# Two MLPs as Strassen quads: seven block products in place of eight, with the residual and the hidden layer in DRAM

## The chip, the cores and the metric

The kernel runs on one core of one Trainium2 chip. The metric is the device time of one execution in microseconds; a median over several executions stands for a kernel. The engines are TensorE (PE, with its weight load PEld), VectorE (DVE), ScalarE (ACT), GpSimd (POOL) and SyncE (SP), which here issues all transfers.

## The reference

Two layers over 1024 tokens of width 1024 in fp32. In each a mixer (another one in each layer), a cross attention on a memory, and an MLP add to the residual `x`; a last norm ends it. The change is in the MLPs (4096 hidden columns):

```python
def rmsnorm(x, g):
    xf = x.astype(jnp.float32)
    y = xf * lax.rsqrt(jnp.mean(xf * xf, axis=-1, keepdims=True) + EPS)
    return (y * g.astype(jnp.float32)).astype(x.dtype)

def sq_relu_mlp(h, w1, w2):
    return jnp.square(jax.nn.relu(h @ w1)) @ w2

    for l in range(DEPTH):
...
        x = x + mem_cross_attn(rmsnorm(x, xa_norm[l]), memn, xa_wq[l], xa_wk[l], xa_wv[l], xa_wo[l])
        x = x + sq_relu_mlp(rmsnorm(x, mlp_norm[l]), mlp_w1[l], mlp_w2[l])
    return rmsnorm(x, final_norm)
```

## The kernel before

Everything is feature-major: a tile is 128 features by 512 tokens, and the tokens come in two halves. The residual is 16 such tiles, which stay in SBUF from the first addition of a layer to its end. fp32 operands are split into two parts, `hi` (a cast to fp32r on ScalarE) and `lo` (the source minus `hi`, a subtraction), and each 128x128 by 128x512 product is three matmuls: hi·hi, hi·lo, lo·hi (`mm3`, L149 to L151).

Weights come as tiles of 128x1024 (512 KB) through `ldw`: the load, the cast on ScalarE (L142), the subtraction on GpSimd (L143). The program's six parts run one after the other: mix0, xa0 (cross attention), mlp0, mix1, xa1, mlp1 with the last norm.

`mlp` first splits the residual times the gain (`split_half`, L233 and L234; the factor 1/rms is left for later) and makes 1/rms of every token (`norm_stat`: squares L176, their sum L178, a matmul with ones L187, L192, a power on GpSimd L195, the diagonal L207, a matmul L208, and a copy L212 into `yy`). The part for half 0 of the tokens stands first; that for half 1 waits as `pending` while the work on half 0 goes on. Then come eight chunks of 512 hidden columns. In a chunk `up` makes 4 tiles for both halves (8 × 3 matmuls each), takes each out of PSUM with one VectorE operation (L1355: max with 0, times `yy`), squares it (L1359, ScalarE), and splits it (L1361 ScalarE, L1362 VectorE); `down` makes 8 output tiles for both halves (4 × 3 matmuls each) and adds them to the residual (L251). That is 192 + 192 = 384 matmuls a chunk, 3072 a layer. `lagged` orders the items so that the second half runs one or two items behind the first. Names in the rows: `hh`/`hl` are the parts of the normed input, `wr`/`wh`/`wl` a weight raw and its parts, `L` the parts of the hidden layer, `mm` a PSUM bank, `x` a residual tile.

The order of instructions on each engine is set by the framework's scheduler, which works with a modelled timeline and lets lines under `high_priority()` go first. On the chip each engine, and SP's list of transfers, runs its list in order.

Of the kernel before, what the change touches and what calls it, by code (L numbers as in the profile page):

```python
# [26 lines left out]
class Model:  # L27
    def __init__(self, ctx, tc, a):
        self.tc, self.nc, self.a = tc, tc.nc, a
        self.const = ctx.enter_context(tc.tile_pool(name="const", bufs=1))  # L30
# [150 lines left out]
    def rms(self, xs, n, ss, eng, scale=1.0):  # L181
        """scale / rms of every token, tokens on partitions: a column for each 128."""
# [15 lines left out]
    def norm_stat(self, xs, n, bank, eng, copy=True):  # L198
        """1/rms of every token, on all partitions (by a product with a diagonal) and as rms() has it."""
# [53 lines left out]
    def lagged(self, items, load, do, head=1, tail=1):  # L253
        """do(item, tile, half) for both halves, the second one an item behind (head and tail: at the ends)."""
# [13 lines left out]
    def proj(self, w, half, tag=None):  # L268
        """[128 columns, 512 tokens] in PSUM: w holds [128, 8, 128]."""
# [7 lines left out]
    # ---------------------------------------------------------------- pieces  # L277
# [60 lines left out]
    def mix_start(self, l, bank, right):  # L338
        """hT and 1/rms, and the residual's place to the tags in right."""
# [34 lines left out]
    def ab_consts(self):  # L374
# [8 lines left out]
        # neg_tri[s', s] = -1 for s' >= s  # L383
# [4 lines left out]
        # mask_diag[s, t] = -1e30 for s >= t  # L388
# [26 lines left out]
    def scaled(self, t, ps, half, scale=1.0):  # L415
        """t = scale * ps / rms."""
# [3 lines left out]
    def spill(self, i, w, half, scale=1.0, fn=None, tag=None):  # L420
        """One projected tile, through fn(t), to DRAM scratch."""
# [11 lines left out]
    def out_parts(self, gated):  # L433
        """The heads' outputs in parts, where hT was."""
# [32 lines left out]
    # ---------------------------------------------------------------- mLSTM  # L467
    def ml_gates(self):
# [30 lines left out]
        # tanh(x / 15) = 1 - 2 / (exp(2 x / 15) + 1)  # L499
# [21 lines left out]
        # running maximum of a within each chunk, chunks and heads on partitions  # L521
# [11 lines left out]
        # maxima carried from chunk to chunk, on one partition  # L533
# [22 lines left out]
        # w_old of head 2p on partitions 0-63 and of head 2p+1 on 64-127  # L556
# [30 lines left out]
    def ml_heads(self, p):  # L587
        nc = self.nc
        C = None
        for half in HALVES:  # L590
# [3 lines left out]
            for i in range(4):  # L594
# [3 lines left out]
                # queries of the two heads on a diagonal of blocks, keys, queries for the state  # L598
# [104 lines left out]
    # ---------------------------------------------------------------- stick breaking  # L703
# [29 lines left out]
    def sb_attn(self, h):  # L733
# [3 lines left out]
        for Q in HALVES:  # L737
# [9 lines left out]
            for j in range(4 * Q + 3, -1, -1):  # L747
# [10 lines left out]
                # softplus(z) = max(z, 0) + log(1 + exp(-|z|))  # L758
# [46 lines left out]
    # ---------------------------------------------------------------- gated delta rule  # L805
# [34 lines left out]
        # what a doubling from 32 to 64 and one from 64 to 128 multiplies, zero outside of the blocks  # L840
# [3 lines left out]
        # DRAM blocks with a row pitch that makes the diagonal blocks of 32 a regular pattern  # L844
# [13 lines left out]
    def c_gate(self, h):  # L858
        """A head's gate, for the first four heads already times the head's output."""
# [17 lines left out]
    def c_gates(self):  # L877
# [33 lines left out]
        # log of the decay: -exp(a_log) softplus(a + dt)  # L911
# [12 lines left out]
        # a quarter, as the norms are those of doubled keys  # L924
# [20 lines left out]
    def gdn_head(self, h):  # L945
        """Projections of a head, and what precedes its recurrence."""
# [509 lines left out]
```

## Time and profile before

| What | Value |
|---|---|
| Median of 3 runs | 3332.48 us (3332.34 to 3332.71) |
| Span of the profiled execution | 3330.1 us |
| Device time outside the span (median minus span) | 2.4 us |
| TensorE busy | 3208.1 us, 96% of the span |
| VectorE busy | 1622.5 us, 49% |
| ScalarE busy | 1063.6 us, 32% |
| GpSimd busy | 971.6 us, 29% |
| Mean granted TensorE clock | 0.980 of full speed |

The span is counted from the first to the last instruction of one profiled execution, and durations in the rows below come from that execution. A matmul's row gives its modelled duration (0.39 us); since matmuls are pipelined, what one costs is the distance between the starts of two.

### The profile page before, as it was taken

How to read it: one execution, taken by the hardware profiler on the slowest of the kernel's cores; microseconds unless marked ns; L12 is line 12 of the kernel's file. 1: busy time of each engine (PE TensorE's matmuls, PEld its weight loads, DVE VectorE, ACT ScalarE, POOL GpSimd, SP SyncE). 2: the span in 40 equal slices, each digit the busy share in tenths (PEclk: the TensorE clock that was granted, in tenths of full speed). 3: DMA queues.
4: the chain of work that ended last, by engine and by line, in shares of the span. 5: the costliest groups of instructions: out<-in, count | busy, mean ns of one | idle time of the engine just before them, and what ended most of it. 6: DMA issues, size and time to landing. Idle time of an engine off the chain costs nothing. (4 is left out here: it accounts for less than half of the span.)

```text
span 3330.1 us, 39471 instructions
## 1 busy us (share of the span) xinstructions
PE 3208.1 (96%) x15215; PEld 2644.7 (79%) x15215; DVE 1622.5 (49%) x2753; ACT 1063.6 (32%) x2109; POOL 971.6 (29%) x669
## 2 busy tenths in 40 slices
PE   8999889999999999999988999899999999999998
PEld 7777677888788888887777788787888788888886
DVE  5567574545433322326777776453544533223235
ACT  3254563433222221123444343253433322211212
POOL 3355474222122222222343232144222122222221
PEclk9999899999999999999999999999999999999999
DMA  4333452111011111113345556474111011111111
GB/s 149 114 110 106 155 199 74 51 48 42 27 50 51 51 45 45 51 45 122 87 119 147 149 170 201 152 253 141 51 39 51 26 51 51 45 45 51 45 51 64
DMA packets 215372, 293.29 MB, mean 88 GB/s; under 512 B 32176, under 2 KB 140944, under 8 KB 215184
## 3 DMA queue, kind: packets, MB, share of 16 engines
q1 hardware_dynamic: 215184, 290.77, 28.6%
q8 instruction: 120, 1.97, 0.2%
q14 instruction: 68, 0.56, 0.1%
HBM read 223.01 MB, written 67.70 MB: 87 GB/s over the span
## 5 line engine op out<-in xcount | busy, mean ns | idle before, releaser
L143 POOL TENSOR_TENSOR wl<-wr,wh 128x1024 fp32r<-128x1024 f32 x248 | 609.9, 2460 | 1508.4 <-ACT wh L142 1492.4
L149 PE MATMUL mm<-hh,wh 128*128 128x512 f32 x2400 | 952.0, 397 | 8.4 <-DVE x L251 3.7
L150 PE MATMUL mm<-hl,wh 128*128 128x512 f32 x2400 | 953.2, 397 | 0.0
L151 PE MATMUL mm<-hh,wl 128*128 128x512 f32 x2400 | 950.9, 396 | 0.0
L142 ACT CAST wh<-wr 128x1024 fp32r<-128x1024 f32 x248 | 260.2, 1049 | 984.2 <-PE mm L150 873.9
L251 DVE TENSOR_TENSOR x<-mm,x 128x512 f32<-128x512 f32 x416 | 286.1, 689 | 563.0 <-PE mm L151 561.8
L149 PEld LDWEIGHTS mm<-hh,wh 128*128 128x128 f32 x2400 | 456.3, 190 | 105.6 <-issue 6.6
L151 PEld LDWEIGHTS mm<-hh,wl 128*128 128x128 f32 x2400 | 456.6, 190 | 93.6 <-issue 0.9
L150 PEld LDWEIGHTS mm<-hl,wh 128*128 128x128 f32 x2400 | 457.0, 190 | 93.1 <-DVE hl L461 0.4
L149 PE MATMUL mm<-L,wh 128*128 128x512 f32 x1024 | 404.8, 395 | 0.0
L151 PE MATMUL mm<-L,wl 128*128 128x512 f32 x1024 | 404.5, 395 | 0.0
L150 PE MATMUL mm<-L,wh 128*128 128x512 f32 x1024 | 404.4, 395 | 0.0
L1362 DVE TENSOR_TENSOR L<-t,L 128x512 fp32r<-128x512 f32 x128 | 160.3, 1253 | 168.7 <-ACT L L1361 168.6
L1355 DVE SCALAR_TENSOR_TENSOR t<-mm,yy 128x512 f32<-128x512 f32 x128 | 88.5, 691 | 312.4 <-PE mm L151 312.4
L151 PEld LDWEIGHTS mm<-L,wl 128*128 128x128 f32 x1024 | 192.2, 188 | 46.6
L150 PEld LDWEIGHTS mm<-L,wh 128*128 128x128 f32 x1024 | 192.2, 188 | 46.4
L149 PEld LDWEIGHTS mm<-L,wh 128*128 128x128 f32 x1024 | 192.2, 188 | 46.3
L1359 ACT ACTIVATE t<-t 128x512 f32<-128x512 f32 x128 | 80.3, 628 | 283.5 <-DVE t L1355 283.5
L990 DVE SCALAR_TENSOR_TENSOR t<-raw,convw,t 128x512 f32<-128x512 f32 x144 | 123.0, 869 | 17.6 <-ACT t L988 17.0
L149 PE MATMUL mm<-o,woh 128*128 128x512 f32 x256 | 103.8, 407 | 1.6 <-ACT o L1228 1.6
L150 PE MATMUL mm<-o,woh 128*128 128x512 f32 x256 | 101.2, 395 | 2.7 <-DVE o L1229 2.7
L151 PE MATMUL mm<-o,wol 128*128 128x512 f32 x256 | 100.8, 394 | 0.0
(414 smaller groups left out, 4089.7 us busy)
## 6 DMA issues: line engine op xcount, KB each, us to landing
wr<-in_w SPq DMA_DIRECT2D x128, 512.0 KB, 3.5
B<-Bd SPq DMA_DIRECT2D x64, 384.0 KB, 4.4
wr<-in_c_w SPq DMA_DIRECT2D x32, 512.0 KB, 4.1
wr<-in_ab_w SPq DMA_DIRECT2D x24, 512.0 KB, 3.5
pj<-p SPq DMA_DIRECT2D x48, 256.0 KB, 2.0
x<-in_xT SPq DMA_DIRECT2D x32, 256.0 KB, 5.9
wr<-in_wk SPq DMA_DIRECT2D x16, 512.0 KB, 4.5
wr<-in_wv SPq DMA_DIRECT2D x16, 512.0 KB, 4.8
```

What stands on the lines that cost most here:

```text
L142: nc.scalar.copy(hi, raw)
L143: (eng or nc.gpsimd).tensor_sub(lo, raw, hi.bitcast(F32))
L149: mm(out, w[0], x[0], start=first, stop=False)
L150: mm(out, w[0], x[1], start=False, stop=False)
L151: mm(out, w[1], x[0], start=False, stop=last)
L251: self.nc.vector.tensor_add(x, ps, x)
L990: nc.vector.scalar_tensor_tensor(out=cv, in0=raw[:, j : j + 512], scalar=wj(j), in1=cv, op0=ALU.mult, op1=ALU.add)
L1355: nc.vector.scalar_tensor_tensor(out=r, in0=ps, scalar=0.0, in1=self.y[half], op0=ALU.max, op1=ALU.mult)
L1359: nc.scalar.activation(s, r, AF.Square)
L1362: nc.vector.tensor_sub(lo, s, hi.bitcast(F32))
```

## The change

Both products of the MLP are made as quads. The columns and rows of a product are cut in two by two blocks, and a quad gets the four output blocks from seven block products p1 to p7 (order `ORDER` = 1, 2, 6, 7, 4, 5, 3) in place of eight, with sums and differences of blocks as operands. The parts:

* **Operands of weights** (`a_load`, `a_ops`): each group loads four raw blocks of 128x1024, GpSimd makes four sums of them (128x1024 each), and all seven are split, the cast on ScalarE, the subtraction on VectorE (`halves`, L1387 and L1388). Before, GpSimd subtracted.
* **Operands of the input** (`mlp_h`): both norms are applied first (16 operations, L1440), and seven sets of four 128x512 tiles are made and split. Then the residual goes to DRAM (`x_close(self.xd)`), and the sets for p5 and p3 take its place in SBUF.
* **Up** (`mlp_up`): 8 groups of 7 products × 2 column blocks × 12 matmuls. Products accumulate in a chain of additions from PSUM; relu and square are on ScalarE; three more sums (GpSimd L1539, L1543, L1545, VectorE L1540) make the operands of the next product's quads, and seven tiles go to DRAM (`mlp_put`), for each q of two.
* **Down** (`mlp_down`): 4 rounds `c` of 14 slots × 2 × 12 matmuls. An operand set of 128x2048 (1 MB) is loaded from DRAM (`b_load`) and split into four; the residual is loaded back (`x_open`), and products are added to it. `V1` and `V3` hold two partial sums until the last round.
* The pools `wp` and `res` are closed for the MLP and opened again after it. The layouts of `w1` and `w2` follow the blocks.

In all 7 × 384 = 2688 matmuls a layer take the place of 3072.

```diff
     def mlp(self, l, out=None):
-        with self.phase(dict(sc=2), L=22):
-            self.split(4 + l, self.rms_rows)
-            self.mlp_chunks(l)
...
+        self.base.close()
+        self.xd = self.dr.tile([NK, 128, 1024], F32, tag=f"xd{l}", name=self.nm("xd"))
...
+            self.aw = self.lpool(st, "aw")
+            with ExitStack() as up:
+                self.ao = self.lpool(up, "ao")
+                self.wt = self.lpool(up, "wt")
+                self.mlp_up(l, up)
+            with ExitStack() as down:
+                self.mlp_down(l, down)
...
+    def halves(self, pool, src, n, th, tl, nh, eng=None):
...
+        nc.scalar.copy(hi, src)
+        (eng or nc.vector).tensor_sub(lo, src, hi.bitcast(F32))
...
+    def a_ops(self, raw, pool):
...
+        x = self.aw.tile([128, 1024], F32, tag="x", name=self.nm("s2"), bufs=1)
+        yield split(raw[11])
+        gp.tensor_add(raw[11], raw[11], raw[21])
+        gp.tensor_add(x, raw[11], raw[22])
+        yield split(raw[12])
+        yield split(x)
+        gp.tensor_add(raw[12], raw[12], x)
+        yield split(raw[11])
+        gp.tensor_add(raw[21], raw[21], raw[22])
+        yield split(raw[22])
+        yield split(raw[21])
+        yield split(raw[12])
...
+    def mlp_h(self, l, up):
...
+        self.y[0] = stat(0)
+        for k in range(4):
+            h11[k], h21[k] = norm(k, 0), norm(4 + k, 0)
+            put(1, k, h11[k])
+        for k in range(4):
+            put(2, k, h21[k])
+        self.y[1] = stat(1)
+        for k in range(4):
+            h12[k], h22[k] = norm(k, 1), norm(4 + k, 1)
+            t3, n2 = self.tmp(), self.tmp()
+            nc.vector.tensor_sub(t3, h22[k], h12[k])
+            nc.vector.scalar_tensor_tensor(out=n2, in0=t3, scalar=-1.0, in1=h11[k], op0=ALU.mult, op1=ALU.subtract)
+            put(6, k, n2)
+            put(7, k, t3)
+            nc.gpsimd.tensor_add(h21[k], h21[k], n2)
+            nc.gpsimd.tensor_sub(h12[k], h11[k], h12[k])
+            put(4, k, h21[k])
+        self.x_close(self.xd)
...
+        for k in range(4):
+            put(5, k, h12[k])
+        for k in range(4):
+            put(3, k, h22[k])
...
+                    with self.tc.high_priority():
+                        if p == 1:
+                            t[q] = w()
+                            nc.scalar.copy(t[q], ps)
+                        elif p == 2:
+                            b11[q] = w()
+                            self.relu2(b11[q], ps)
+                        elif p == 6:
+                            u[q] = w()
+                            nc.vector.tensor_add(u[q], ps, t[q])
...
+                    elif p == 3:
+                        self.relu2(u[q], u[q])
+                        t3, n2 = self.tmp(), self.tmp()
+                        nc.gpsimd.tensor_sub(t3, t[q], u[q])
+                        nc.vector.scalar_tensor_tensor(
+                            out=n2, in0=t3, scalar=-1.0, in1=b11[q], op0=ALU.mult, op1=ALU.subtract
+                        )
+                        nc.gpsimd.tensor_sub(u[q], b11[q], u[q])
+                        t4 = w()
+                        nc.gpsimd.tensor_add(t4, b22[q], n2)
+                        for pp, z in ((7, t3), (6, n2), (5, u[q]), (4, t4)):
+                            self.mlp_put(g, q, pp, z)
```

Three places where the lists of the engines differ. **TensorE, where an MLP begins (mlp0).** Before, three tiles of half 0 (72 matmuls, the last two of them the first rows here) stand ahead of the statistic of half 1 (L187, L208):

```order
L150 MATMUL mm_1721_7914<-hl_1661_7711,wh_1719_7910 128x512
L151 MATMUL mm_1721_7914<-hh_1660_7710,wl_1720_7911 128x512
L187 MATMUL sc_1698_7827<-ones_78,acc_1699_7828 128x1 x4
L208 MATMUL sc_1698_7827<-t_1708_7858,ones_78 128x128 x4
L149 MATMUL mm_1726_7947<-hh_1682_7795,wh_1675_7758 128x512
L150 MATMUL mm_1726_7947<-hl_1683_7796,wh_1675_7758 128x512
```

Behind it come tiles of half 1 (`hh_1682`). In the changed kernel 24 matmuls (p1 of both column blocks) stand ahead of it; L192 and L213 are its two matmuls there. `ga` is the bank of p1 and p2, `gb` of p6 and p7, `mm` of p4:

```order
L213 MATMUL gc_1729_7843<-t_1739_7874,ones_72 128x128 x4
L1425 MATMUL gb_1813_8109<-hi_1745_7893,hi_1799_8029 128x512
L1425 MATMUL gb_1815_8124<-hi_1745_7893,hi_1799_8029 128x512
L1425 MATMUL mm_1826_8182<-hi_1749_7903,hi_1807_8069 128x512
L1425 MATMUL mm_1828_8200<-hi_1749_7903,hi_1807_8069 128x512
L1426 MATMUL gb_1813_8109<-lo_1746_7894,hi_1799_8029 128x512
L1427 MATMUL gb_1813_8109<-hi_1745_7893,lo_1800_8030 128x512
L1426 MATMUL gb_1815_8124<-lo_1746_7894,hi_1799_8029 128x512
L1427 MATMUL gb_1815_8124<-hi_1745_7893,lo_1800_8030 128x512
L1425 MATMUL gb_1813_8109<-hi_1755_7915,hi_1799_8029 128x512
L1425 MATMUL gb_1815_8124<-hi_1755_7915,hi_1799_8029 128x512
L1425 MATMUL ga_1803_8038<-hi_1721_7827,hi_1686_7734 128x512
```

Behind the statistic the first ten matmuls now take operands of half 1 (`hi_1745`, `lo_1746`, `hi_1749`, `hi_1755`), and the eleventh, the first of p2, accumulates in the bank `ga_1803` that p1 has filled.

**ScalarE at the same place.** Before:

```order
L1361 CAST L_1680_7791<-t_1679_7789 128x512
L176 ACTIVATE t_1703_7839<-x_1202_5260 128x512
L176 ACTIVATE t_1704_7842<-x_1203_5262 128x512
L176 ACTIVATE t_1705_7845<-x_1204_5264 128x512
L176 ACTIVATE t_1706_7848<-x_1205_5266 128x512
L1359 ACTIVATE t_1715_7902<-t_1714_7900 128x512
L1361 CAST L_1716_7904<-t_1715_7902 128x512
L1359 ACTIVATE t_1723_7941<-t_1722_7939 128x512
L1361 CAST L_1724_7943<-t_1723_7941 128x512
```

That is a cast of the hidden layer, squares of half 1, and then again work on hidden tiles. After, where L1511 copies p1 out of its bank:

```order
L1387 CAST hi_1747_7897<-t_1743_7889 128x512
L1387 CAST hi_1745_7893<-t_1744_7890 128x512
L1387 CAST hi_1783_7997<-h_1741_7885 128x512
L1387 CAST hi_1757_7919<-t_1753_7911 128x512
L1387 CAST hi_1749_7903<-h_1706_7797 128x512
L1387 CAST hi_1755_7915<-t_1754_7912 128x512
L1387 CAST hi_1785_8001<-h_1751_7907 128x512
L1387 CAST hi_1767_7941<-t_1763_7933 128x512
L1387 CAST hi_1759_7925<-h_1710_7805 128x512
L1511 COPY w_1804_8051<-ga_1803_8038 128x512
L1387 CAST hi_1787_8005<-h_1761_7929 128x512
L1511 COPY w_1806_8066<-ga_1805_8053 128x512
```

The two copies of p1 now stand behind nine casts of operands of half 1; two of these sources (`h_1706`, `h_1710`) are sums that GpSimd makes from operands of half 1, and `h_1741` and `h_1751` differences.

**SP's transfers, from up to down (mlp0).** Before there is no such place, and weights follow on weights:

```order
L138 DMA wr_1718_7908<-in_w1 128x1024
L138 DMA wr_1736_8013<-in_w1 128x1024
L138 DMA wr_1754_8118<-in_w2 128x1024
L138 DMA wr_1759_8152<-in_w2 128x1024
L138 DMA wr_1766_8214<-in_w2 128x1024
```

Each of them waits only for a place in the pool of raw weights. After: `xd` is the residual's copy in DRAM, `hd` the hidden layer's sets there, `r11` to `r22` raw blocks of `w2` for the second pair of column blocks, `br` the 1 MB sets on their way back (`hd_1648` is p2's set of the first round):

```order
L1556 DMA hd_1672_7704<-w_2114_10226 128x512
L76 DMA x_2179_10390<-xd_1646_7678 128x512
L1396 DMA r11_2180_10392<-in_w2 128x1024
L1556 DMA hd_1671_7703<-t_2115_10247 128x512
L1556 DMA hd_1670_7702<-t_2116_10248 128x512
L1396 DMA r12_2181_10394<-in_w2 128x1024
L1556 DMA hd_1673_7705<-w_2103_10104 128x512
L1396 DMA r21_2182_10396<-in_w2 128x1024
L1556 DMA hd_1672_7704<-w_2117_10252 128x512
L1396 DMA r22_2183_10398<-in_w2 128x1024
L1578 DMA br_2212_10508<-hd_1651_7683 128x2048
L1578 DMA br_2135_10299<-hd_1648_7680 128x2048
```

The first raw block of the second pair (`r11_2180`) now stands behind the residual's loads and behind puts of the last group, and the load of p2's set behind the last of these puts.

## Rows read from the trace of the kernel before

**Rows 1.** The page: span; busy us, share and instructions by engine; GB/s in 40 slices.

```profile
span 3330.1 us, 39471 instructions
...
PE 3208.1 (96%) x15215; PEld 2644.7 (79%) x15215; DVE 1622.5 (49%) x2753; ACT 1063.6 (32%) x2109; POOL 971.6 (29%) x669
...
GB/s 149 114 110 106 155 199 74 51 48 42 27 50 51 51 45 45 51 45 122 87 119 147 149 170 201 152 253 141 51 39 51 26 51 51 45 45 51 45 51 64
```

**Rows 2.** Windows, inside the first MLP: busy us and count by engine, PEclk, DMA share, GB/s.

```profile
900.00:1500.00 600.00, 600.00 (x2609) 489.52 (x2609) 178.22 (x217) 120.56 (x160) 129.45 (x54) 1.00 0.16 47
```

**Rows 3.** VectorE's timeline, the same eviction in two consecutive chunks: start us, us, what.

```profile
971.42 0.69 DVE L1355 SCALAR_TENSOR_TENSOR t<-mm,yy 128x512 f32<-128x512 f32 x1 [1.55 <-PE mm L151]
...
1059.74 0.69 DVE L1355 SCALAR_TENSOR_TENSOR t<-mm,yy 128x512 f32<-128x512 f32 x1 [1.55 <-PE mm L151]
```

**Rows 4.** Groups by form, 900 to 1500 us: busy us, mean ns, idle time before.

```profile
L143 POOL TENSOR_TENSOR wl<-wr,wh 128x1024 fp32r<-128x1024 f32 x54 | 129.5, 2397 | 472.5 <-ACT wh L142 472.5
...
L251 DVE TENSOR_TENSOR x<-mm,x 128x512 f32<-128x512 f32 x111 | 76.7, 691 | 214.2 <-PE mm L151 214.2
L1362 DVE TENSOR_TENSOR L<-t,L 128x512 fp32r<-128x512 f32 x53 | 65.8, 1241 | 72.7 <-ACT L L1361 72.7
L142 ACT CAST wh<-wr 128x1024 fp32r<-128x1024 f32 x54 | 56.8, 1052 | 359.9 <-PE mm L150 330.3 <-PE mm L151 29.7
...
L1361 ACT CAST L<-t 128x512 fp32r<-128x512 f32 x53 | 32.9, 621 | 1.7
```

**Rows 5.** Groups by form, the whole program, same columns.

```profile
L1242 POOL TENSOR_TENSOR k<-p,k 128x512 fp32r<-128x512 f32 x8 | 10.4, 1296 | 48.1 <-ACT k L1241 47.5 <-DMA p<-kv 0.6
```

**Rows 6.** GpSimd's timeline at 873 us.

```profile
873.17 2.40 POOL L143 TENSOR_TENSOR wl<-wr,wh 128x1024 fp32r<-128x1024 f32 x1 [9.86 <-ACT wh L142]
```

**Rows 7.** VectorE's timeline at 874 us, and all instances of L1362 (ns min/median/max).

```profile
874.25 1.86 DVE L1362 TENSOR_TENSOR L<-t,L 128x512 fp32r<-128x512 f32 x1 [1.35 <-ACT L L1361]
...
L1362 DVE TENSOR_TENSOR L<-t,L x128: 685/1248/1858, 854.5 to 3268.2; 128x512 fp32r<-128x512 f32 x128
```

**Rows 8.** TensorE's timeline at 834 us: the statistic of half 0 begins.

```profile
834.27 1.02 PE L187 MATMUL sc<-ones,acc 128*128 128x1 f32 x8 [0.18 <-DVE acc L178]
```

**Rows 9.** VectorE's timeline, 835 to 842 us: the end of the cross attention.

```profile
835.34 0.16 DVE L192 TENSOR_SCALAR yc<-sc 128x4 f32<-128x4 f32 x1
...
839.83 0.68 DVE L212 COPY yy<-sc 128x512 f32<-128x512 f32 x1
840.43 0.74 DVE L234 SCALAR_TENSOR_TENSOR hl<-x,gains,hh 128x512 fp32r<-128x512 f32 x1
841.09 0.68 DVE L251 TENSOR_TENSOR x<-mm,x 128x512 f32<-128x512 f32 x1
841.69 0.74 DVE L234 SCALAR_TENSOR_TENSOR hl<-x,gains,hh 128x512 fp32r<-128x512 f32 x1
```

**Rows 10.** TensorE's timeline: the first MLP matmul, and the statistic of half 1.

```profile
844.68 0.39 PE L149 MATMUL mm<-hh,wh 128*128 128x512 f32 x1
...
861.01 0.95 PE L187 MATMUL sc<-ones,acc 128*128 128x1 f32 x8
...
864.96 0.77 PE L149 MATMUL mm<-hh,wh 128*128 128x512 f32 x1
...
868.09 0.41 PE L150 MATMUL mm<-hl,wh 128*128 128x512 f32 x1
```

**Rows 11.** Windows, at the same place: columns as in rows 2.

```profile
865.00:870.00 5.00, 5.00 (x16) 3.98 (x17) 2.56 (x4) 2.41 (x4) 0.00 (x0) 0.69 0.00 0
```

**Rows 12.** TensorE's timeline: the first matmul after the first MLP.

```profile
1559.06 0.47 PE L149 MATMUL mm<-hh,wh 128*128 128x512 f32 x1 [0.30 <-DVE x L251]
```

**Rows 13.** TensorE's timeline: the last matmul of the second MLP.

```profile
3312.20 0.40 PE L151 MATMUL mm<-L,wl 128*128 128x512 f32 x1
```

**Rows 14.** DMA issues: count, KB each, median us to landing.

```profile
wr<-in_w SPq DMA_DIRECT2D x128, 512.0 KB, 3.5
...
x<-x_scratch SPq DMA_DIRECT2D x16, 256.0 KB, 5.5
```

More of the change, by code (lines that the diff above doesn't have):

```diff
@@ L1337, in xa_units @@
                 out(*cur, o)
-    def mlp(self, l, out=None):
-        with self.phase(dict(sc=2), L=22):
-            self.split(4 + l, self.rms_rows)
-            self.mlp_chunks(l)
-            if out is not None:
-                self.finish(out)
-    def mlp_chunks(self, l):
-        nc = self.nc
-        w1, w2 = self.a["w1"], self.a["w2"]
-        for c in range(8):
-            hid = [[None, None] for _ in range(4)]
-            def up(j, w, half):
-                ps = self.proj(w, half)
-                r = self.tmp()
-                nc.vector.scalar_tensor_tensor(
-                    out=r, in0=ps, scalar=0.0, in1=self.y[half], op0=ALU.max, op1=ALU.mult
-                )
-                s = self.tmp()
-                nc.scalar.activation(s, r, AF.Square)
-                hi, lo = self.keep(), self.keep()
-                nc.scalar.copy(hi, s)
-                nc.vector.tensor_sub(lo, s, hi.bitcast(F32))
-                hid[j][half] = (hi, lo)
-            self.lagged(range(4), lambda j: self.ldw(w1[l, 4 * c + j]), up, 2 if c == 0 else 1)
-            def down(j, w, half):
-                hi = w[0].rearrange("p (k c) -> p k c", k=4)
-                lo = w[1].rearrange("p (k c) -> p k c", k=4)
-                for i in range(2):
-                    ps = self.mm_ps()
-                    for k in range(4):
-                        s = slice(i * 128, i * 128 + 128)
-                        self.mm3(ps, (hi[:, k, s], lo[:, k, s]), hid[k][half], k == 0, k == 3)
-                    self.add_res(2 * j + i, half, ps)
-            self.lagged(range(4), lambda j: self.ldw(w2[l, c, j]), down, 1, 1 if c < 7 else 2)
@@ new lines, with lpool @@
+    ORDER = (1, 2, 6, 7, 4, 5, 3)
+    BNAME = {1: "b11", 2: "b21", 6: "n2", 7: "t3", 4: "t4", 5: "n1", 3: "b22"}
+    def lpool(self, stack, name, side=None):
+        kw = dict(side=side) if side else {}
+        return stack.enter_context(self.tc.tile_pool(name=self.nm(name), bufs=1, **kw))
+    def mlp(self, l, out=None):
+        self.base.close()
+        self.xd = self.dr.tile([NK, 128, 1024], F32, tag=f"xd{l}", name=self.nm("xd"))
+        self.hd = [
+            {p: self.dr.tile([128, 2048], F32, tag=f"hd{l}{c}{p}", name=self.nm("hd")) for p in self.ORDER} for c in range(4)
+        ]
+        self.right = {}
+        self.bufs = dict(ga=2, gb=2, gc=2)
+        with ExitStack() as st:
+            self.pp = st.enter_context(self.tc.tile_pool(name=self.nm("pp"), bufs=1, space=PSUM))
+            self.aw = self.lpool(st, "aw")
[5 more added lines that the diff above has]
+                self.mlp_down(l, down)
+                if out is not None:
+                    self.finish(out)
+        if out is None:
+            self.open_base()
@@ new lines, in halves, with a_load @@
+    def halves(self, pool, src, n, th, tl, nh, eng=None):
+        nc = self.nc
+        hi = pool.tile([128, n], F32R, tag=th, name=self.nm("hi"), bufs=nh)
+        lo = pool.tile([128, n], F32R, tag=tl, name=self.nm("lo"), bufs=nh)
+        nc.scalar.copy(hi, src)
+        (eng or nc.vector).tensor_sub(lo, src, hi.bitcast(F32))
+        return hi, lo
+    def a_load(self, src, pools):
+        raw = {}
+        for i, b in enumerate((11, 12, 21, 22)):
+            t = pools[b].tile([128, 1024], F32, tag=f"r{b}", name=self.nm(f"r{b}"), bufs=1)
+            self.nc.sync.dma_start(out=t, in_=src[i])
+            raw[b] = t
+        return raw
@@ new lines, in product, with put, norm @@
+    def product(self, ps, a, q, b, first, last):
+        mm = self.nc.tensor.matmul
+        for k in range(4):
+            s = slice(q * 512 + k * 128, q * 512 + k * 128 + 128)
+            hi, lo = a[0][:, s], a[1][:, s]
+            mm(ps, hi, b[k][0], start=first and k == 0, stop=False, skip_group_check=True)
+            mm(ps, hi, b[k][1], start=False, stop=False, skip_group_check=True)
+            mm(ps, lo, b[k][0], start=False, stop=last and k == 3, skip_group_check=True)
+    def mlp_h(self, l, up):
+        nc = self.nc
+        B = {p: [None] * 4 for p in self.ORDER}
+        pools = {p: self.lpool(up, f"b{p}") for p in (1, 2, 6, 7, 4)}
+        def put(p, k, t):
+            B[p][k] = self.halves(pools[p], t, 512, f"h{k}", f"l{k}", 1)
+        def norm(k, half):
+            t = self.wt.tile([128, 512], F32, tag="w", name=self.nm("h"), bufs=14)
+            nc.vector.scalar_tensor_tensor(
+                out=t, in0=self.x[k][half], scalar=self.gain(4 + l, k), in1=self.y[half], op0=ALU.mult, op1=ALU.mult
+            )
+            return t
+        self.y = [None, None]
+        h11, h21, h12, h22 = ([None] * 4 for _ in range(4))
+        stat = lambda half: self.norm_stat(self.half_x(half), 512, lambda: self.bank("gc"), nc.vector)[0]
+        self.y[0] = stat(0)
[16 more added lines that the diff above has]
+        self.x_close(self.xd)
+        pools[5] = self.lpool(self.mright, "b5", "right")
+        pools[3] = self.lpool(self.mright, "b3", "right")
+        for k in range(4):
+            put(5, k, h12[k])
+        for k in range(4):
+            put(3, k, h22[k])
+        return B
@@ L1381, in finish @@
         for half in HALVES:
-            y = self.norm_stat(self.half_x(half), 512, lambda: self.bank("sc"), nc.vector, False)[0]
+            y = self.norm_stat(self.half_x(half), 512, lambda: self.bank("gc"), nc.vector, False)[0]
             for k in range(NK):
-                o = self.res.tile([128, 512], F32R, tag=f"hh{k}{half}", name=self.nm("o")).bitcast(F32)
                 x, g = self.x[k][half], self.gain(6, k)
-                nc.vector.scalar_tensor_tensor(out=o, in0=x, scalar=g, in1=y, op0=ALU.mult, op1=ALU.mult)
-                nc.sync.dma_start(out=out[k, :, half * 512 : half * 512 + 512], in_=o)
+                nc.vector.scalar_tensor_tensor(out=x, in0=x, scalar=g, in1=y, op0=ALU.mult, op1=ALU.mult)
+                nc.sync.dma_start(out=out[k, :, half * 512 : half * 512 + 512], in_=x)
 @with_exitstack
```

158 lines of the change are left out of this document (153 added, 5 removed).

## Prediction

> **What bounds the kernel now.** I read the page first, then windows inside an MLP, then timelines at the MLP's ends. TensorE is busy for 96% of the span, VectorE for 49% [rows 1]; from 900 to 1500 us, within the first MLP, TensorE is busy all 600 us at a granted clock of 1.00, VectorE 178, ScalarE 121, GpSimd 129, and the transfers run at 47 GB/s [rows 2]. So the MLP is as long as its matmuls. The same eviction comes 1059.74 − 971.42 = 88.32 us later in the next chunk [rows 3]; a chunk is 384 matmuls, so one costs 0.230 us (600 us over 2609 gives the same [rows 2]). The MLP begins at 844.68 without a gap [rows 10] and ends at 1559.06 with 0.30 us of idle time [rows 12]. Only half 1's statistic costs something: from 861.01 to 868.09 TensorE does 7 matmuls, 1.6 us of work, so 5.5 us are lost [rows 10], 1.5 of them because the 7 from 864.96 to 868.09 take 3.1 us at a mean clock of 0.69 [rows 10, 11]. The last matmul starts at 3312.20 [rows 13], and 17.9 us of norm and output follow.
>
> **The gain.** 2688 matmuls replace 3072: 384 fewer a layer, one chunk. As long as TensorE stays the bound, both layers give 2 × 88.32 = 176.6 us. Everything else takes from that.
>
> **Does TensorE stay the bound?** An up group is 168 matmuls, 38.6 us; a down round is 336, 77.3 us. Prices: a subtraction or eviction of 128x512 on VectorE 0.69 us [rows 4, 7], a GpSimd sum of 128x1024 2.40 [rows 4] and of 128x512 1.30 [rows 5], casts on ScalarE 1.05 and 0.62 [rows 4]. A VectorE subtraction of 128x1024 is not in the trace: at least 0.69, at most twice that, 1.38; since the fixed part of a small operation is within 0.16 (the 128x4 one) [rows 9], I take 2 × 0.69 − 0.16 = 1.22.
> - Up group: VectorE 7 × 1.22 + 12 × 0.69 = 16.8 us; GpSimd 4 × 2.40 + 6 × 1.30 = 17.4. Even if the two never overlapped, 34.2 is below 38.6. ScalarE: 7 × 1.05 + 2 copies + 16 activations at 0.62 is 18.5.
> - Down round: VectorE 14 × 1.22 + 28 splits × 0.69 + 28 evictions × 0.69 = 55.7; GpSimd 8 × 2.40 = 19.2. Together 74.9, below 77.3. ScalarE: 14 × 1.05 + 28 × 0.62 = 32.
> - Transfers: 5.8 MB in a group and 11.5 MB in a round, 149 GB/s; one slice of the trace moved 253 [rows 1].
>
> The two engines do stand in each other's way: a GpSimd subtraction ran from 873.17 for 2.40 us [rows 6], VectorE's L1362 started at 874.25, took 1.86 and ended 0.54 after it [rows 7]; alone it takes 0.69, the smallest of its 128 instances [rows 7], while its mean is 1.24 [rows 4]. Evictions from PSUM (L251) keep 0.69 although GpSimd is busy for a fifth of that time [rows 2, 4]. The Trainium skill ("SBUF — State Buffer", section "Who interferes with whom") states that a VectorE instruction with two SBUF inputs and a GpSimd one that reads SBUF exclude each other, and that the second blocks fully; this trace agrees, and by that rule VectorE would need at most 55.7 + 19.2 us a round.
>
> In the mean it holds, but every list runs in order. Walking through the lists of a steady group with these prices, operands of weights are ready some 3 us or more before TensorE wants them, and an eviction has 24 matmuls (5.5 us) before its bank is added to. A round has less room: 77.3 − 74.9 = 2.4 us in the worst case. I charge one subtraction (1.22) for each of 8 rounds: **10 us** (0 if hidden; the upper end is the second rival).
>
> **Where an MLP begins.** This is the largest cost. Before, 72 matmuls (16.6 us) cover half 1's statistic; now 24 (5.5 us) do, and all behind them needs half 1. With the cross attention unchanged, `yy` of half 0 is there at 839.83 + 0.68 = 840.5 [rows 9]. VectorE then has 25 operations to the end of half 1's squares, back to back at 0.66 for 8 with two operators and at 0.60 for 17 (the distances of the starts from 840.43 [rows 9]): 15.5, so 856.0. From the statistic's first matmul at 834.27 [rows 8] to the copy's end at 840.5 are 6.2 us: `yy` of half 1 at 862.2. Six norms, a difference and its double operation follow, 5.3: 867.5. The copy of p1 stands on ScalarE behind casts whose sources come from 4 GpSimd sums (5.2) and 7 more VectorE operations (4.3); with two inputs from SBUF on both sides I take them one after the other: 877, and p2 can start at 878. The remaining 22 VectorE operations (14.4) and 4 sums (5.2) end at 896.6, and 28 matmuls (6.4) are left then: 903.0. Unstalled, p1, p2, p6, p4 and p5 (120 matmuls, 27.6 us from 844.68) would end at 872.3. So 30.7 us are lost; the four raw sums on GpSimd (4 × 2.40) delay operations in the attention's tail, for which I add 2.4; the clock falls after idle time as it did before, 1.5 [rows 10, 11]; and 5.5 that were lost before go. Net 29, for two layers **58 us** (30 to 72: at the lower end sums and VectorE overlap wholly, −2 × 10.4, and TensorE catches up in between; at the upper the raw sums delay the tail in full, +2 × 7.2).
>
> **From up to down.** The residual's half 1 can be loaded only when p3, up's last product, has released its operands (time T). On SP the first raw block of the second pair stands behind these loads and behind puts. A 512 KB load takes 3.5 us, a 256 KB one of the residual 5.5 [rows 14]; I put its landing at T + 4.4, so with cast and subtraction (1.05 + 1.22) its product can begin at T + 6.7, while TensorE has matmuls only until T + 1.8: 4.9 us. Then 48 matmuls (11.0) run to T + 17.7. p2's set (1 MB, between 3.5 and 2 × 3.5 us) waits for the last put, which follows three GpSimd sums and a VectorE operation (about 4.6 us) behind p3's eviction, relu and square; with put, load and split it is there at about T + 18.5: 0.8 more. With 1.5 for the clock it is 7 a layer, **14 us** (6 to 30).
>
> **From the MLP on.** The pools of weights open again only after the MLP, so the first `ldw` of mix1 waits for a place: about **2 us** (0 to 5, a load and its split) where 0.30 was idle before. The last norm is the same work: 0.
>
> **Sum.** 176.6 − 58 − 14 − 2 − 10 = 92.6. From its span, 3330.1 − 92.6 = 3237.5; the median lies 2.4 above the span: **3240 us**. A difference of 0.2% (6.7 us) is about what a measurement can tell from no change.
>
> **Rivals.**
> - *Starts better covered.* The scheduler's lists follow a modelled timeline; if VectorE and GpSimd overlap at the start, an MLP's start costs 14 and up to down 3 each, the rest 7: 176.6 − 28 − 6 − 7 = 135.6, so 3197. For it: evictions are not slowed by GpSimd [rows 4]. Against: the casts ahead of p1's copy need half 1 anyhow.
> - *VectorE binds in places.* If every subtraction of a round took what L1362 takes in the mean, a round would be 14 × 2.48 + 28 × 1.24 + 28 × 0.69 = 88.8 us of VectorE, 11.5 over TensorE's: 8 × 11.5 = 92 in place of 10, so 3322; with half of it 3280. For it: L1362 nearly doubles beside a GpSimd that is busy only 22% of the time [rows 2, 4]. Against: what VectorE waits for GpSimd cannot be more than GpSimd is busy, 19.2 a round, by which the sum above stays below TensorE's; and before each L1362 VectorE had idle time (72.7 us for 53) [rows 4].
> - *Slower: the queue of transfers.* SP issues in order, and a group's puts wait for its last sums; the next group's raw loads can stand behind them. If nothing covers that, a group pays the chain load, two sums, cast and subtraction: 3.5 + 4.8 + 1.05 + 1.22 = 10.6 us, 16 × 10.6 = 170, so 3410. It decides from 92.6 + 6.7 = 99.3 over 16 = 6.2 us a group. For it: transfers rise from 47 to 149 GB/s. Against: in the list the raw loads of a group come 4 to 10 us before their sums are wanted.
> - *No change to be told.* The losses sum to the gain by accident, 3326 to 3339.
>
> **Chances.** Forecast 0.60 (its own range 3218 to 3266), starts better covered 0.13, VectorE binding 0.15, no change 0.04, slower 0.08. Faster is 0.60 + 0.13 + 0.15 = 0.88. The range from 3185 to 3315 leaves out slower and no change (0.12), and some 0.08 at the far ends of the VectorE case and of the better start.
>
> **What would show it.** 768 matmuls fewer, and starts 0.23 apart in mid-group at a clock of 1.00. A gap behind the 24th matmul of each MLP, in two pieces, of 30 us in all, released by ScalarE and VectorE rather than by a transfer. Two gaps at up to down, released by a split and by a transfer. VectorE 17 us busy in a group and 56 in a round, more where GpSimd works. The prediction is wrong if gaps of a few us stand in every group or round (then VectorE, or SP's queue, by what releases them), if the 128x1024 subtraction takes over 1.38 us, or if p1's copy comes before half 1's statistic.

## The result, and the profile after

The changed kernel takes 3256.39 us (median of four runs, 3247.44 to 3264.27), before 3332.41; the ratio is 0.9775 with a 95% interval of 0.9756 to 0.9793. It is faster by 76 us, inside the range; the forecast was 3240. The page of its profile, as in [rows 1], and two groups of it:

```profile
span 3253.9 us, 39918 instructions
...
PE 3049.9 (94%) x14447; PEld 2513.9 (77%) x14447; DVE 2054.7 (63%) x3161; ACT 1312.3 (40%) x2501; POOL 1237.5 (38%) x813
...
L1388 DVE TENSOR_TENSOR lo<-r,hi 128x1024 fp32r<-128x1024 f32 x192 | 287.4, 1500 | 143.0 <-ACT hi L1387 140.9
...
L1408 POOL TENSOR_TENSOR r<-r,r 128x1024 f32<-128x1024 f32 x32 | 82.7, 2584 | 515.5 <-DVE lo L1388 471.3
```

TensorE has 768 matmuls less, and its busy share falls from 96% to 94%: the MLPs' middle is as dense as before, their ends are not. Four windows of the changed kernel (columns as in [rows 2]): an up group, the gap from up to down, a down round, and the start of mix1:

```profile
917.38:955.96 38.58, 38.58 (x169) 31.54 (x168) 20.85 (x21) 18.55 (x28) 20.63 (x10) 1.00 0.46 163
1193.00:1207.00 14.00, 0.25 (x2) 0.20 (x2) 5.30 (x6) 2.99 (x5) 8.40 (x6) 0.58 0.98 327
1280.31:1356.47 76.16, 76.16 (x338) 63.06 (x337) 57.95 (x71) 30.16 (x42) 20.21 (x8) 1.00 0.42 152
1513.90:1537.40 23.50, 19.65 (x97) 16.12 (x95) 18.97 (x43) 9.11 (x17) 5.17 (x9) 0.99 0.43 136
```

Group and round have no idle time at all. At mix1's start VectorE is busy 19.0 us of 23.5; the same 72 matmuls and half 1's statistic took 18.4 us before, with VectorE busy 10.2, as this window of the kernel before shows:

```profile
1559.00:1577.40 18.40, 18.34 (x89) 15.38 (x90) 10.23 (x23) 3.56 (x6) 6.22 (x9) 1.00 0.69 207
```

The first MLP's beginning on TensorE: the first of the attention's last 18 score matmuls, the attention's last matmul, the two sides of the wait for half 1, and the 121st matmul of the MLP.

```profile
812.23 0.28 PE L154 MATMUL sc<-k,q 128*128 128x256 f32 x1
...
856.92 0.63 PE L156 MATMUL mm<-o,wol 128*128 128x512 f32 x1
...
862.21 0.39 PE L1427 MATMUL ga<-hi,lo 128*128 128x512 f32 x1
...
874.33 1.22 PE L1425 MATMUL gb<-hi,hi 128*128 128x512 f32 x2 [6.86 <-ACT hi L1387]
...
906.44 0.40 PE L1425 MATMUL gb<-hi,hi 128*128 128x512 f32 x1
```

From 812.23 to 856.92 are 44.7 us; before, the same stretch took 31.2 (813.28 to 844.45). VectorE (first three rows) and GpSimd (last two) show why:

```profile
818.58 1.75 DVE L1275 SCALAR_TENSOR_TENSOR s<-s,yc 128x2 f32<-128x2 f32 x1
...
820.91 4.38 DVE L1286 TENSOR_SCALAR t<-t,s 128x256 f32<-128x256 f32 x2
...
825.39 2.24 DVE L1286 TENSOR_SCALAR t<-t,s 128x256 f32<-128x256 f32 x1
```

```profile
817.24 3.06 POOL L1408 TENSOR_TENSOR r<-r,r 128x1024 f32<-128x1024 f32 x1 [14.45 <-DMA r<-in_w]
820.38 2.39 POOL L1409 TENSOR_TENSOR s<-r,r 128x1024 f32<-128x1024 f32 x1
```

Softmax normalisations of 128x256 (L1286), 0.35 us in the median, take over 2 us each while the raw sums run. At up to down, on TensorE (the last matmul of up's last product, the two sides of the gap), then in SP's list, then the GpSimd sum that the put of 1198.53 waits for and ScalarE's cast that waits for the block:

```profile
1190.80 0.40 PE L1427 MATMUL gc<-hi,lo 128*128 128x512 f32 x1
...
1192.65 0.40 PE L1427 MATMUL ga<-hi,lo 128*128 128x512 f32 x1
1206.80 0.79 PE L1425 MATMUL gb<-hi,hi 128*128 128x512 f32 x1 [13.75 <-ACT hi L1387]
```

```profile
1198.53 0.32 SPq L1556 DMA_DIRECT2D hd<-w  x1
...
1199.45 0.57 SPq L1396 DMA_DIRECT2D r<-in_w  x1
```

```profile
1196.86 1.64 POOL L1545 TENSOR_TENSOR w<-w,t 128x512 f32<-128x512 f32 x1 [1.23 <-DVE t L1540]
```

```profile
1205.70 1.04 ACT L1387 CAST hi<-r 128x1024 fp32r<-128x1024 f32 x1 [10.76 <-DMA r<-in_w]
```

The first raw block of the second pair is issued at 1199.45, 8.7 us after the last matmul of up's last product started (1190.80), behind a put that waited for a GpSimd sum until 1198.50. The load then took 6.2 us, where 3.5 was the median before: the transfers' share is 0.98 there (second window above). And the end: half 0's outputs (L1653) stand ahead of half 1's last two sums on VectorE, and behind the last matmul (3230.99).

```profile
3232.76 5.35 DVE L1653 SCALAR_TENSOR_TENSOR x<-x,gains,gc 128x512 f32<-128x512 f32 x8
3238.03 1.48 DVE L183 TENSOR_TENSOR acc<-acc,t 128x512 f32<-128x512 f32 x2
```

Before, the same eight outputs began 5.1 us ahead of the start of the last matmul (3312.20):

```profile
3307.06 5.36 DVE L1386 SCALAR_TENSOR_TENSOR o<-x,gains,sc 128x512 f32<-128x512 f32 x8 [0.20 <-PE sc L208]
```

### The profile page after: what moved, and what is told of

The parts are those of the page before. It is cut to its first block, busy times and chain, and to the rows that moved or that the text cites. A ratio compares the mean times of both kernels' runs of the same rounds, so it can differ in the third digit from the quotient of the medians.

```text
span 3253.9 us, 39918 instructions
## 1 busy us (share of the span) xinstructions
PE 3049.9 (94%) x14447; PEld 2513.9 (77%) x14447; DVE 2054.7 (63%) x3161; ACT 1312.3 (40%) x2501; POOL 1237.5 (38%) x813
## 4 chain that ended last, share of the span: by engine, by line
PE 34%; DVE 8%; issue 4%; DMA 4%; POOL 2%; ACT 1%; SPq 0%; POOLq 0%; DVEq 0%; ACTq 0%
PE mm L154 4%; PE mm L155 4%; PE mm L156 4%; PE gc L1427 2%; PE gc L1425 2%; PE gc L1426 2%; PE ga L1426 1%; PE gb L1426 1%; PE gb L1427 1%; PE ga L1427 1%; PE ga L1425 1%; PE gb L1425 1%; DVE t L995 1%; DVE lo L1388 1%; DMA M<-gr 1%
## 5 line engine op out<-in xcount | busy, mean ns | idle before, releaser
L154 PE MATMUL mm<-hh,wh 128*128 128x512 f32 x1376 | 552.1, 401 | 6.9 <-DVE s L1018 1.9
L155 PE MATMUL mm<-hl,wh 128*128 128x512 f32 x1376 | 553.3, 402 | 0.0
L156 PE MATMUL mm<-hh,wl 128*128 128x512 f32 x1376 | 551.3, 401 | 0.0
L148 POOL TENSOR_TENSOR wl<-wr,wh 128x1024 fp32r<-128x1024 f32 x120 | 301.5, 2514 | 440.2 <-ACT wh L147 437.7
L1388 DVE TENSOR_TENSOR lo<-r,hi 128x1024 fp32r<-128x1024 f32 x192 | 287.4, 1500 | 143.0 <-ACT hi L1387 140.9
L1387 ACT CAST hi<-r 128x1024 fp32r<-128x1024 f32 x192 | 201.1, 1050 | 269.1 <-PE gc L1426 94.7
L155 PEld LDWEIGHTS mm<-hl,wh 128*128 128x128 f32 x1376 | 264.1, 192 | 52.9 <-DVE hl L466 0.4
L1388 DVE TENSOR_TENSOR lo<-br,hi 128x512 fp32r<-128x512 f32 x224 | 202.1, 917 | 29.1 <-ACT hi L1387 28.5
L1425 PE MATMUL gc<-hi,hi 128*128 128x512 f32 x512 | 201.4, 394 | 4.6 <-DVE x L1638 4.5
L1427 PE MATMUL gc<-hi,lo 128*128 128x512 f32 x512 | 201.6, 395 | 0.3 <-DVE lo L1388 0.3
L1426 PE MATMUL gc<-lo,hi 128*128 128x512 f32 x512 | 201.6, 394 | 0.0
L1387 ACT CAST hi<-br 128x512 fp32r<-128x512 f32 x224 | 134.2, 619 | 158.5 <-PE mm L1427 84.4
```

Source lines behind the costliest of these rows:

```text
L148: (eng or nc.gpsimd).tensor_sub(lo, raw, hi.bitcast(F32))
L1387: nc.scalar.copy(hi, src)
L1388: (eng or nc.vector).tensor_sub(lo, src, hi.bitcast(F32))
L1425: mm(ps, hi, b[k][0], start=first and k == 0, stop=False, skip_group_check=True)
L1426: mm(ps, hi, b[k][1], start=False, stop=False, skip_group_check=True)
L1427: mm(ps, lo, b[k][0], start=False, stop=last and k == 3, skip_group_check=True)
```

## The experiments

Runs of one kernel differ by up to 21 us (e3: 3249.8 to 3270.5), those of before by 13 (3329.0 to 3342.1), more than the 6.7 us that the prediction took a measurement to tell apart. So stages of the traces are compared, one trace for each kernel. **Tail**: from the attention's last 18 score matmuls to its last matmul. **Start**: from there to the MLP's 121st matmul. **Up to down**: from the 1344th to the 1512th matmul, less a group's 38.6 us. **End**: from the last MLP matmul to the span's end. Two values are the two layers; before had 31.2 / 32.2 for the tail, 33.1 for the start's work (27.6 and the 5.5 of the prediction), and 17.9 for the end. Times are medians of two to five runs. Kernels whose edit does not touch a stage show its spread: tails of 42.8 to 44.8, starts of 49.5 to 54.0, up to down of 15.7 to 17.9.

| Kernel | Time | Tail | Start | Up to down | End |
|---|---|---|---|---|---|
| changed | 3256.4 | 44.7 / 43.9 | 49.5 / 51.0 | 16.3 / 16.0 | 22.9 |
| again (e12) | 3260.4 | 44.4 / 42.8 | 53.0 / 52.9 | 16.4 / 16.2 | 22.9 |
| e1, raw sums on VectorE | 3252.9 | 41.2 / 41.4 | 49.9 / 51.0 | 16.5 / 16.1 | 23.0 |
| e2, no raw sums | 3247.0 | 37.3 / 37.3 | 53.5 / 51.0 | 15.7 / 16.4 | 23.0 |
| e3, p1 and p2 early | 3260.8 | 44.1 / 42.9 | 52.1 / 52.2 | 16.5 / 16.6 | 22.9 |
| e4, residual later | 3256.6 | 43.7 / 42.9 | 51.0 / 51.8 | 16.9 / 17.3 | 23.0 |
| e5, half 1 gated | 3256.2 | 44.4 / 44.0 | 53.0 / 51.4 | 14.6 / 15.0 | 22.9 |
| e6, all start sums on VectorE | 3246.7 | 41.2 / 40.7 | 46.7 / 46.4 | 17.9 / 16.2 | 22.9 |
| e7, subtractions twice | 3318.1 | 42.8 / 43.4 | 51.7 / 54.0 | 21.3 / 21.4 | 24.4 |
| e8, outputs behind | 3250.7 | 44.8 / 43.2 | 52.0 / 52.7 | 17.0 / 16.1 | 21.4 |
| e9, combined | 3227.0 | 41.1 / 40.1 | 45.0 / 47.0 | 10.7 / 10.5 | 21.4 |
| e10, e9 and e3 | 3226.3 | 41.2 / 40.6 | 45.1 / 46.6 | 11.9 / 10.3 | 21.4 |
| e11, e9 and raw sums | 3226.1 | 41.3 / 40.5 | 45.1 / 46.6 | 8.9 / 9.3 | 21.4 |

**e1: the first group's raw sums on VectorE.**

```diff
...
-                    gen[0] = self.a_ops(self.a_load(w1[i // 7], aw), self.ao)
+                    gen[0] = self.a_ops(self.a_load(w1[i // 7], aw), self.ao, nc.vector if i == 0 else None)
```

> The four raw sums of an MLP's first group are made by VectorE in place of GpSimd, in both layers; all else as in the changed kernel (3256 us). Theory: in the cross attention's tail VectorE is held up by GpSimd's four sums of 128x1024, among them normalisations of 128x256 that take 0.35 us in the median and up to 2.44; without them some 7 us of waits go and 4 x 1.2 us of work come, so 2 to 4 us less a layer, 3248 to 3252, and no normalisation takes over 0.5 us. Rival: the tail is late because VectorE has too much work of its own there; then 4.9 us more work a layer makes it 3261 to 3266.

The tail is 3 us shorter a layer although VectorE has 4.9 us more to do, so it was GpSimd's blocking that cost more than the work. The longest normalisation is 1.36 us, as in the kernel before, not under 0.5. The time, 3252.9, is 1 us over the theory's range.

**e2: no raw sums in the first group.**

```diff
+        if not sums:
+            for b in (11, 12, 22, 11, 22, 21, 12):
+                yield split(raw[b])
+            return
...
```

> The first group's four raw sums are left out in both layers, and raw blocks are split in their place (so the MLPs' first group is another product); the number of splits, matmuls and transfers stays. Theory (GpSimd's sums hold VectorE up in the tail): the end of the cross attention moves forward by 7 to 10 us a layer, 3236 to 3242. Rival (VectorE's own work): within 3 us a layer, 3250 to 3256.

7.0 us a layer less in the tail (44.3 to 37.3 in the mean of both): the sums cost that much there. The time, 3247.0, lies between the two ranges; in the first layer the start gave 4 us back, and the starts of the two traces of the unchanged kernel differ by 3.5 there. Of the other 5.6 over before, part is a wait of 2.26 us at 849.29 for an eviction that stands behind five norms (3.40 us) in VectorE's list; in the whole tail VectorE is busy 3.6 us more (32.8 against 29.2). No run takes these apart further.

**e3: p1 and p2 ahead of half 1's statistic.**

```diff
...
+        first = group(0)
+        next(first)
+        next(hgen)
+        for _ in first:
+            pass
...
```

> The products p1 and p2 of the first group stand in the program ahead of half 1's statistic and norm, so that 48 matmuls lie ahead of its wait and p1's copies ahead of half 1's casts on ScalarE. Theory: p2's 24 matmuls (5.5 us) fill idle time, and the end of the start's 120 matmuls moves forward by about 5 us a layer: 3244 to 3248. Rival: the start ends when VectorE has made the last operands of half 1, whatever TensorE does before; then 3254 to 3258 and the gap only moves.

The rival, in the stage; the time, 3260.8, is above both ranges, in the kernel with the widest spread. The wait moved behind the 48th matmul and shrank by half (from 12.1 us between two starts to 5.6), as this row of it shows, but the start is not shorter: it still ends with the last operands of half 1.

```profile
879.31 0.79 PE L1425 MATMUL gb<-hi,hi 128*128 128x512 f32 x1 [5.34 <-ACT hi L1387]
```

**e4 and e5: the residual's loads behind the raw blocks; half 1's gated besides.**

```diff
         b_load(2)
-        self.x_open(self.xd)
         a_prep(2)
+        self.x_open(self.xd)
...
+                if gate is not None:
+                    self.nc.gpsimd.tensor_copy(t[:, 0:1], gate[:, 0:1])
...
+            if s == 2:
+                self.x_open(self.xd, (1,), raws[1])
```

The first part is e4; e5 has half 0 alone in that place, and the two other parts.

> The residual's loads stand in the program behind the raw blocks of the second pair, so that on SP these blocks come ahead of the last eight loads and of the last group's puts. Theory (order of SP's queue): the first raw block is issued some 6 us earlier, the gap of 14 us from up to down shrinks to 6 to 8 and a second one of 0 to 3 stays before p2: 3242 to 3248. Rival (rate of the transfers: 327 GB/s at a share of 0.98 from 1193 to 1207 us): what comes first only pushes the rest back, and the gap moves to p2's set: 3253 to 3257.

> As the run with the residual's loads behind the raw blocks, and half 1's eight loads (2.1 MB) besides wait, by a tiny GpSimd copy into each tile, for p2's set to be there. Theory (from up to down the transfers' rate binds, 327 GB/s): 2.1 MB less ahead of p2's set is 6.4 us, so up to down loses 9 to 11 us a layer in place of 16.5, and the program is at 3243 to 3248. Rival (p2's set waits for the chain of sums and puts that ends the last group, whatever else is loaded): 14 to 17 us a layer, 3252 to 3258.

The rivals' numbers, both times. In e4 the first raw block is issued at 1197.23, before TensorE runs dry. The first gap falls from 13.9 to 3.8 us, and new ones of 1 to 3 us follow, with matmuls at a mean granted clock of 0.53 (1203 to 1212 us) between. In e5 2.1 MB less ahead of p2's set make the stage 2.3 us shorter than in e4, not 6.4. The second gap there is not a wait for p2's set, as the rival had it: TensorE waits for a weight sum of p6 that GpSimd finishes at 1217.62, behind the last group's sums:

```profile
1211.93 3.38 POOL L1416 TENSOR_TENSOR r<-r,r 128x1024 f32<-128x1024 f32 x1
1215.27 2.35 POOL L1411 TENSOR_TENSOR s<-r,r 128x1024 f32<-128x1024 f32 x1
```

```profile
1218.75 0.50 PE L1427 MATMUL mm<-hi,hi 128*128 128x512 f32 x1 [3.05 <-ACT hi L1389]
```

So several limits lie there behind one another: SP's order, which alone gives nothing (e4), the transfers (2.3 us), and GpSimd's list.

**e6: the input's sums on VectorE too.**

```diff
-            nc.gpsimd.tensor_add(h21[k], h21[k], n2)
-            nc.gpsimd.tensor_sub(h12[k], h11[k], h12[k])
+            nc.vector.tensor_add(h21[k], h21[k], n2)
+            nc.vector.tensor_sub(h12[k], h11[k], h12[k])
```

> In both layers the first group's raw sums and the eight sums of the input's operands (h21 + n2 and h11 - h12) are made by VectorE in place of GpSimd. Theory (at the start the two engines shut each other out: these sums take GpSimd 1.6 to 7.0 us each in place of 1.3): from the cross attention's end to the 120th matmul it is 43 to 46 us in place of 49.5 and 51, and the attention ends 6 us earlier: 3230 to 3240. Rival (the start is as long as VectorE's own work, now 5.5 us more): 50 to 56 us, 3244 to 3256.

The theory's direction at a smaller size: 46.7 and 46.4 against 49.5 to 54.0. The attention ends 3 us earlier, not 6, and the time, 3246.7, lies in the rival's range. More work on one engine takes less time here than the same work on two that shut each other out. Undisturbed, the operation that the trace of before lacked has this price:

```profile
L1388 DVE TENSOR_TENSOR lo<-r,hi 128x1024 fp32r<-128x1024 f32 x4 | 4.9, 1220 | 0.2 <-ACT hi L1387 0.2
```

**e7: every weight subtraction of down done twice.**

```diff
+        if self.twice and n == 1024:
+            nc.vector.tensor_sub(lo, src, hi.bitcast(F32))
```

> In the down product every subtraction of a weight operand (128x1024) is done twice, into the same tile: 14 x 1.22 = 17 us more VectorE work a round. VectorE is busy for 58 us of a round's 76 now. Theory (lists in order bind only when an engine is near full): a round takes 76 to 79 us, 3256 to 3285 in all. Rival (VectorE binds in places long before): 82 us or more a round, over 3300.

3318.1 us, a time of the rival's range; middle rounds take 80.1 and 81.2 us, between the two, while first and last rounds pay more (5 and 10 to 12 us each). A window of about one round has VectorE busy for 98% of it:

```profile
1310.00:1391.00 81.00, 77.21 (x333) 63.09 (x332) 79.59 (x85) 30.44 (x42) 21.27 (x8) 0.98 0.42 143
```

In a middle round VectorE binds when it is full and hardly before: of the reserve of 18 us (76.2 less 58.0) some 12 can be used.

**e8: half 0's outputs behind half 1's sum.**

```diff
...
+        nc.vector.tensor_scalar_mul(g[:, 8:9], self.acc[:, 0:1], 0.0)
+        nc.vector.tensor_scalar(
+            out=g[:, 0:8], in0=self.gains[:, 48:56], scalar1=g[:, 8:9], scalar2=0.0, op0=ALU.add, op1=ALU.add
+        )
...
```

> At the program's end half 0's eight outputs take their gain from a tile that is written after half 1's squares are summed (gain plus zero times that sum), so that VectorE makes them behind that sum. Theory: the statistic of half 1 waits for two sums that stand behind these eight outputs (5.3 us) on VectorE; the end after the last matmul falls from 22.9 to 17 to 19 us. Rival: the outputs are only moved behind the statistic, and the end stays at 22 to 24 us.

Nearly the rival: the sums come 5 us sooner, but all sixteen outputs (10.6 us) now follow the statistic; the end is 21.4 us, 1.5 less, outside both ranges.

**e9 to e11: combined.** To e6, e5 and e8 comes that the last up group's sums run on VectorE; e10 adds e3, e11 the first down round's raw sums on VectorE.

```diff
+                        eng = nc.vector if g == 7 else nc.gpsimd
-                        nc.gpsimd.tensor_sub(t3, t[q], u[q])
+                        eng.tensor_sub(t3, t[q], u[q])
...
```

> Together: the first group's raw sums and the input's sums on VectorE, the last up group's three sums for each q on VectorE too, the raw blocks ahead of the residual's half 1 whose loads wait for p2's set, and the outputs' gain tile at the end. Theory (from up to down the rest of the wait is GpSimd's list: last group's sums, then raw sums, each shut out by VectorE's subtractions): up to down loses 9 to 11 us in place of 16, the start stays at 46.5, 3228 to 3236. Rival (VectorE is full there, so its 4 us more take the gain back): 14 to 18 us, 3240 to 3248.

> The combined version with p1 and p2 of the first group ahead of half 1's statistic besides. Theory (the start ends with VectorE's last operand of half 1): from the cross attention's end to the 120th matmul 46 to 48 us, as without. Rival (with GpSimd out of the way TensorE's order counts): 41 to 43 us, 8 to 10 us less in all.

> The combined version with the raw sums of the first down round on VectorE as well (8 x 1.22 us of VectorE in place of 8 x 2.4 of GpSimd). Theory (GpSimd's list binds from up to down): 2 to 4 us less there than in the combined version. Rival (VectorE is full there): 2 to 6 us more.

The theories, nearly each time: e9's time is 1 us below its range, e10's starts (45.1 and 46.6) are as long as e9's, and e11 gains 1.8 and 1.3 us a layer there, 3.1 in both, where 2 to 4 were expected. With the last group's sums off GpSimd, up to down loses 10.6 us in place of the 14.8 of e5, and 9.1 in e11, where GpSimd has no sum left there; e10's early products give nothing again. e9 takes 3227.0 us, 0.9675 of before (0.9662 to 0.9688), e11 3226.1 (0.9671, 0.9658 to 0.9685): both beat the kernel before and the changed one, and cannot be told from each other. What is left from up to down begins with a gap of 4.7 us in e11:

```profile
1186.23 0.40 PE L1427 MATMUL ga<-hi,lo 128*128 128x512 f32 x1
1191.33 0.79 PE L1425 MATMUL gb<-hi,hi 128*128 128x512 f32 x1 [4.70 <-ACT hi L1390]
```

**e12: the changed kernel again.**

> The changed kernel once more, unchanged, for the spread that its own runs have: up groups 280.9 us from the 120th to the 1344th matmul and down rounds of 76.2 us as before to 0.2 us; what differs from run to run lies outside the MLPs' steady parts.

The steady parts repeat (280.9 us from the 120th to the 1344th matmul in both layers of both traces). The spread comes from elsewhere: the attention's last scores start at 819.01 here and at 812.23 in the first run, with the same work ahead of them.

## Why the prediction was right, and where its terms were off

- **The gain (176.6) and its condition.** Right: TensorE stays the bound inside groups and rounds. A group takes 38.58 us (38.6 forecast), a round 76.16 (77.3, since a matmul costs 0.227 there). VectorE's work was 20.9 and 58.0 us (16.8 and 55.7 without waits), and its 128x1024 subtraction costs 1.22 undisturbed, as estimated. In the mean it takes 1.50, over the 1.38 that was named as a sign of being wrong; what comes on top is waiting for GpSimd, which the sum of both engines had allowed for.
- **The charge for rounds (10).** At the wrong place: middle rounds lose nothing; the last ones take 5.1 and 3.5 us more, which the faster matmuls give back. By e7 the reserve of middle rounds is real.
- **Where an MLP begins (58).** Right in its sum, 59.5: tails 13.5 and 11.7, starts 16.4 and 17.9. Its parts were off (2.4 and 26.7 a layer were charged), and that the errors cancel is luck. Reckoned as the prediction did it, by VectorE's copy of `yy`: the copy of half 0 ended 35.25 and 34.47 us after the start of the attention's last 18 scores, where it had been 27.23 and 28.28; that is 8.0 and 6.2 later, charged with 2.4, and GpSimd's raw sums alone cost the tail 7 (e2). From there the steps came as forecast or sooner: in the first layer `yy` of half 1 after 20.7 us (forecast 21.7), p2 after 35.8 (37.5), released by p1's copy as forecast, the 120th matmul after 58.7 (62.5, and 1.5 for the clock); in the second 22.8, 37.8 and 60.2. Behind the 24th matmul stand one gap of 12.1 us and several of 0.1 to 1.6, not two. The rows of the first layer stand below this list.
- **What held up the tail and the start.** The price of a blocked operation was looked up for subtractions only, while normalisations with one tensor and a column of factors are blocked too. The Trainium skill ("SBUF — State Buffer", section "Who interferes with whom") lists tensor_scalar among the operations that can take the shared port; the 2.24 us of L1286 beside the sums, against 0.35, agree. The second part of the start's step, that p1's copy behind half 1's casts costs time, fell with e3 and e10: the last operands of half 1 end the start in any case.
- **From up to down (14).** Mis-sized: 32.3. The step "I put its landing at T + 4.4" failed: with T at 1190.80 the raw block was issued only at T + 8.7, behind a put that waited for GpSimd's sums, and its cast began at T + 14.9, since the load took 6.2 us beside the other transfers. The put's chain had been priced for p2's set, but not for the block that stands in the same queue. That is not the whole of it: in e4 the block comes early and the stage is as long, and only with GpSimd's sums on VectorE besides (e9, e11) is it 5.5 to 7.4 us shorter.
- **From the MLP on (2), the end (0).** Mis-sized: 9.6 and 5.0. mix1's first 18.4 us became 23.5, with waits released by VectorE (splits, statistic), not by weights. The rest, between 4 and 5 us, lies inside mix1 and stays open: from the first MLP's last matmul to the second attention's last scores, traces with the same mix1 range over 8 us (1010 to 1018; 1025 in e7). At the end half 0's outputs (5.3), before covered by the last matmuls, stand behind them and ahead of two sums; e8, which only moves them, wins 1.5.
- **The sum.** 176.6 − 59.5 − 32.3 − 9.6 − 5.0 = 70.2. Each MLP before took 713.7 us from its first to its last matmul, 1.6 more than eight chunks of 88.32 and 5.5, and the first attention came 1.1 earlier: 74.5, of the 76.2 between the profiled spans.

```profile
846.79 0.69 DVE L217 COPY yy<-gc 128x512 f32<-128x512 f32 x1
...
867.50 0.69 DVE L217 COPY yy<-gc 128x512 f32<-128x512 f32 x1 [0.66 <-PE gc L213]
```

```profile
883.25 0.79 PE L1425 MATMUL ga<-hi,hi 128*128 128x512 f32 x1 [0.41 <-ACT w L1511]
```

The rival of starts better covered did not come true (29.9 and 29.6 us a layer, not 14, and 16 at up to down, not 3). Nor did the one in which VectorE binds (e7 shows how near it lay), nor the slower one with SP's queue in every group; that queue held TensorE up once a layer, at up to down, with other limits behind it.

## What to carry to other kernels

Here a saving of matmuls in a dense stage arrived in full, with the other engines' sums below TensorE's even if they exclude each other; its price was paid where stages meet. So cost each seam by every queue that is crossed, each with everything that stands ahead in it. Where VectorE and GpSimd both read operands from SBUF, moving GpSimd's sums to VectorE can shorten a stretch in which VectorE is the bound (e1, e6). Where several limits lie behind one another, taking one away shows little: e4 shortened up to down by nothing, e5 by 1.0 and 1.7 us, e9 and e11 by 5.5 to 7.4 a layer.

## What was not expected of the hardware

A GpSimd sum of 128x512, 1.3 us undisturbed, took 7.01 us while VectorE ran subtractions back to back:

```profile
886.44 7.01 POOL L1462 TENSOR_TENSOR h<-h,t 128x512 f32<-128x512 f32 x1 [3.17 <-DVE t L1459]
```

```profile
889.23 2.49 DVE L1388 TENSOR_TENSOR lo<-h,hi 128x512 fp32r<-128x512 f32 x4
```

VectorE's four, and five more operations with two SBUF inputs ahead of and behind them, ran at their usual 0.60 us distance meanwhile: a train of VectorE operations can hold GpSimd off for several of its own lengths, and an operand made there comes that much later. Seven of the nine traces that keep these sums on GpSimd have such a sum of 7.0 us; in e12 the longest takes 3.9, in e3 1.73.
